# The order of an S5 branch in a three-branch token mixer: tables in two places, scan beside other products

## The chip, the cores and the metric

The kernel runs on one core of a Trainium2 chip. The metric is the device time of one execution in microseconds. TensorE has two clock levels, 1.2 and 2.4 GHz; the profile gives the granted clock as a share of full speed.

## The reference

One layer of a diffusion backbone: 256 latent tokens and 256 context tokens of width 2048, weights in fp32. Both are modulated, projected by one wide matrix `w_in`, and go through three branches of width 768: Hyena (long convolution), mLSTM (scores and states over chunks of 64), and S5 (a complex diagonal state space model). The branches are gated, merged, projected by `w_out`, normalised, and a squared-ReLU MLP of width 8192 follows. The change concerns the S5 branch:

```
SPLIT_SIZES = ((HY_ORDER + 1) * W_HY, 2 * W_ML, W_ML, W_ML, 4 * ML_HEADS, W_S5, N_BRANCH * D_MODEL)
mag = jnp.exp(dt * a_re)
ab_re, ab_im = mag * jnp.cos(dt * a_im), mag * jnp.sin(dt * a_im)
...
bu_re = jnp.einsum('blgc,gpc->blgp', u, bb_re)          # and bu_im
_, _, s_re, s_im = lax.associative_scan(s5_combine, (a_re, a_im, bu_re, bu_im), axis=1)
y = (jnp.einsum('blgp,gcp->blgc', s_re, c_re) - jnp.einsum('blgp,gcp->blgc', s_im, c_im))
```

It runs forward and backward, with 48 groups of 16 channels and 64 states.

## The kernel before

**Weights.** Every matrix streams from HBM in chunks of 512 KB (`wr`, four buffers, SP's queue). ScalarE copies a chunk to a high part `wh` (L190), VectorE makes the low part `wl` by subtraction (L194), three buffers each; TensorE then does three matmuls of 256 columns per 128 x 128 piece (L211), hi x hi, hi x lo, lo x hi, into the PSUM tile `mm`. 24 such matmuls per chunk and token stream, 192 per block of a latent projection.

**Order.** After each chunk `chunk_done` (L216) advances up to three generators, `sides[0]` to `sides[2]`, at a rate given with each. A scheduler then fixes the order on every engine from a timeline of its own. So the rates and the order of calls in `run` set what stands beside what, loosely.

**Stages.** First the modulation blocks (L394), the modulated activations (`h_group`, L427) and parts of the K projection, with `s5_params` (L440) and `s5_tables` (L540) as side. Then V, Q, `mlstm`, U (the S5 inputs), O, 36 chunks of the hyena columns HY, 96 chunks of the merge gates MG, hyena, three merges, `w_out` and the MLP.

**S5.** The sequence is cut into 32 chunks of 8 tokens for each of the two streams. `s5_tables` makes powers times B (`WA`, into the state), powers times C (`QD`, out of the state) and a short kernel (`KK`), 6 column tiles x 2 halves x 2 directions; `powers` (L524) is four multiplications and an addition, on VectorE for the forward and on GpSimd for the backward direction. Tables go to DRAM. `s5_spread` (L594) lays `KK` out as `KD` by eight DMAs of GpSimd's queue. `s5_inject` (L616) multiplies inputs by `WA`; `s5_scan` (L645) runs 63 steps of four operations on GpSimd, each dependent on the one before; `s5_output` (L658) multiplies states by `QD` (L687) and inputs by `KD` (L693), for six column tiles; GLU follows. Before, inject starts after six chunks of HY, the scan runs beside the rest of HY and MG, and the output step stands beside MG. B, C and the powers stay in SBUF while the tables are made.

**Names.** `aux` is a PSUM tile with two buffers; `b2`, `b4`, `t32`, `ty`, `t6` are SBUF tiles by size; `s5Q`, `s5t`, `s5w` are tables being made; `s5wq` and `s5tp` hold tables read back; `sc1`, `sc2` are the scan's temporaries; `mac` is the accumulator of the late modulation, VectorE's work on `wr` (L1181).

## Time and profile before

| | us |
|---|---|
| three runs | 2031.67, 2040.69, 2040.85; median 2040.69 |
| profiled execution, its own time | 2046.25 |
| its span | 2044.3 |
| TensorE busy | 1885.0 (92%) |
| VectorE busy | 1342.6 (66%) |
| ScalarE busy | 797.7 (39%) |
| GpSimd busy | 473.4 (23%) |
| moved from and to HBM | 455.92 MB, mean 223 GB/s |

The last matmul of K ends at 235.0 us and V's first starts at 242.2; V ends at 335.8, Q at 383.7, U at 459.8, O at 520.6, HY at 662.4, MG at 1049, the merges at 1177, `w_out` at 1274, the first MLP product at 1479, the second at 2028. The scan lasts from 634.4 to 807, the output step to 858.

Busy shares are averages; the trace is to be read by stages. Idle time of an engine that is not the last one waited for costs nothing.

### The profile page before, as it was taken

The page shows a single profiled execution, that of the slowest core. Times are in us where ns is not written, and L with a number is a line of the kernel's source. Part 1 is how long each engine was busy: PE and PEld are TensorE (multiplying, and loading weights), DVE is VectorE, ACT ScalarE, POOL GpSimd, SP SyncE. Part 2 cuts the span into 40 slices and gives each one's busy share as a digit, 9 for nine tenths or more (in the row PEclk, how much of TensorE's full clock was granted, in tenths as well). Part 3 has the DMA queues.
Part 4 walks back from the last instruction along what each step waited for, and adds up shares of the span by engine and source line. Part 5 has one row for each costly group of instructions (what it writes and reads, how often), then busy time and mean ns, then how long its engine had stood idle before and what let it go on. Part 6 is the DMA issues. An engine that isn't in the chain of part 4 may idle for free.

```text
span 2044.3 us, 34693 instructions
## 1 busy us (share of the span) xinstructions
PE 1885.0 (92%) x13945; PEld 1716.5 (84%) x13945; DVE 1342.6 (66%) x1842; ACT 797.7 (39%) x1079; POOL 473.4 (23%) x654
## 2 busy tenths in 40 slices
PE   4787899999999896999889998899999999999996
PEld 1555888898998896999769977899989899998986
DVE  8789876655876564455777767866655555555556
ACT  1233333324544332534333443544343334444332
POOL 4777311000015997000343400500000000000001
PEclk8898899999999898999999999999999999999998
DMA  8798667766698675777756876577765566666653
GB/s 311 262 299 285 195 203 221 228 199 184 206 318 272 211 242 172 262 251 243 270 183 217 278 249 218 174 248 229 244 208 190 189 185 181 184 185 230 190 187 115
DMA packets 255200, 455.92 MB, mean 223 GB/s; under 512 B 28789, under 2 KB 75541, under 8 KB 253504
## 3 DMA queue, kind: packets, MB, share of 16 engines
q1 hardware_dynamic: 221824, 382.43, 59.0%
q0 software_dynamic: 12384, 44.54, 6.2%
q10 hardware_dynamic: 20832, 26.75, 3.9%
q8 instruction: 109, 1.79, 0.4%
q14 instruction: 51, 0.42, 0.1%
HBM read 424.75 MB, written 32.05 MB: 223 GB/s over the span
## 4 chain that ended last, share of the span: by engine, by line
PE 64%; DVE 14%; DMA 8%; POOL 8%; issue 4%; ACT 1%; ACTq 0%; POOLq 0%; DVEq 0%; SPq 0%
PE mm L211 57%; DMA wr<-in_w_mod_dram 4%; PE aux L211 4%; DVE wl L194 4%; POOL sc L654 2%; POOL sc L653 2%; POOL t L655 2%; POOL sc L652 2%; DVE t L194 1%; DMA wr<-in_w_in_dram 1%; DVE ty L435 1%; ACT wh L190 1%; DVE mac L1181 1%; DVE s5t L537 1%; DMA s5wq<-WA 1%
## 5 line engine op out<-in xcount | busy, mean ns | idle before, releaser
L211 PE MATMUL mm<-t,wh 128*128 128x256 f32 x5888 | 1102.7, 288 | 24.8 <-ACT wh L190 12.6
L211 PEld LDWEIGHTS mm<-t,wh 128*128 128x128 f32 x5888 | 933.7, 194 | 46.6 <-ACT wh L190 13.9
L194 DVE TENSOR_TENSOR wl<-wr,wh 128x1024 fp32r<-128x1024 f32 (+1 forms) x517 | 657.0, 1277 | 381.6 <-ACT wh L190 380.7
L211 PE MATMUL mm<-t,wl 128*128 128x256 f32 x2944 | 850.1, 289 | 23.3 <-DVE wl L194 23.0
L190 ACT ACTIVATE wh<-wr 128x1024 fp32r<-128x1024 f32 (+1 forms) x517 | 546.4, 1058 | 807.9 <-PE mm L211 577.6
L211 PEld LDWEIGHTS mm<-t,wl 128*128 128x128 f32 x2944 | 571.4, 194 | 37.4 <-DVE wl L194 29.4
L1181 DVE SCALAR_TENSOR_TENSOR mac<-wr,vecs,mac 128x512 f32<-128x512 f32 x240 | 186.8, 778 | 152.7 <-DMA wr<-in_w_mod_dram 150.0
L211 PE MATMUL mm<-wh,t 128*128 128x512 f32 (+1 forms) x960 | 249.3, 349 | 1.7 <-ACT wh L190 1.7
L211 PEld LDWEIGHTS mm<-wh,t 128*128 128x128 f32 x960 | 169.7, 191 | 25.6 <-ACT wh L190 2.7
L211 PE MATMUL mm<-wl,t 128*128 128x512 f32 (+1 forms) x480 | 169.2, 352 | 5.2 <-DVE wl L194 5.2
L211 PE MATMUL mm<-wh,ff 128*128 128x512 f32 (+1 forms) x576 | 155.3, 358 | 0.0
L211 PEld LDWEIGHTS mm<-wh,ff 128*128 128x128 f32 x576 | 101.8, 188 | 17.6
L211 PEld LDWEIGHTS mm<-wl,t 128*128 128x128 f32 x480 | 91.6, 191 | 21.7 <-DVE wl L194 10.5
L211 PE MATMUL mm<-wl,ff 128*128 128x512 f32 (+1 forms) x288 | 103.0, 357 | 0.0
L1403 POOL DMA_DIRECT2D t<-in_ln_g_dram x1 | 0.5, 535 | 358.8 <-PE mm L211 358.8
L211 PE MATMUL mm<-ty,wh 128*128 128x256 f32 x384 | 74.1, 291 | 0.0
L211 PE MATMUL mm<-ty,wl 128*128 128x256 f32 x192 | 57.0, 297 | 6.7 <-DVE wl L194 6.7
L211 PEld LDWEIGHTS mm<-ty,wh 128*128 128x128 f32 x384 | 61.6, 195 | 0.9
L211 PEld LDWEIGHTS mm<-wl,ff 128*128 128x128 f32 x288 | 54.2, 188 | 8.8
L1192 POOL DMA_DIRECT2D mrow<-b x8 | 4.0, 502 | 227.8 <-DVE b L1190 227.8
L211 PE MATMUL aux<-t,t 128*128 128x384 f32 (+3 forms) x160 | 48.8, 422 | 8.0 <-DVE t L1147 3.5
L406 PE MATMUL px<-wr,b 128*32 128x512 f32 x128 | 40.3, 714 | 12.9 <-DVE s5t L335 10.7
(389 smaller groups left out, 1813.6 us busy)
## 6 DMA issues: line engine op xcount, KB each, us to landing
wr<-in_w_ff_dram SPq DMA_DIRECT2D x256, 512.0 KB, 3.9
wr<-in_w_in_dram SPq DMA_DIRECT2D x192, 512.0 KB, 4.7
wr<-in_w_mod_dram SPq DMA_DIRECT2D x160, 512.0 KB, 4.8
wr<-in_w_out_dram SPq DMA_DIRECT2D x32, 512.0 KB, 4.9
wh<-in_w_mod_dram SPq DMA_DIRECT2D x16, 512.0 KB, 6.2
wl<-in_w_mod_dram SPq DMA_DIRECT2D x16, 512.0 KB, 7.8
QD<-s5Q POOLq DMA_DIRECT2D x24, 256.0 KB, 4.9
WA<-s5wa ACTq DMA_DIRECT2D x24, 256.0 KB, 5.2
```

Source lines behind the costliest of these rows:

```text
L190: return self.nc.scalar.activation(out, in_, f, bias=bias, scale=scale)
L194: self.nc.vector.tensor_sub(lo, x, hi.bitcast(F32))
L211: self.nc.tensor.matmul(out, lhsT, rhs, start=start, stop=stop, skip_group_check=True)
L406: nc.tensor.matmul(ps[o:o + 32], self.st[:, k, :], raw[:, kk, :], start=k < 4, stop=k >= KT - 4, skip_group_check=True, tile_position=(0, o))
L435: self.nc.vector.tensor_scalar(h[:, j], h[:, j], self.modc[:, 16 + k, m:m + 1], self.modc[:, k, m:m + 1], op0=ALU.mult, op1=ALU.add)
L537: e.tensor_mul(t[:, :, s], bcp(s), bcm(1))
L652: v.tensor_mul(t1, self.a8[:, 0], S[:, :, :, :, n - 1])
L653: v.tensor_mul(t2, self.a8[:, 1], S[:, :, ::-1, :, n - 1])
L654: v.tensor_add(t1, t1, S[:, :, :, :, n])
L655: v.tensor_add(S[:, :, :, :, n], t1, t2)
L1181: v.scalar_tensor_tensor(acc, x, c, acc, op0=ALU.mult, op1=ALU.add)
L1192: nc.gpsimd.dma_start(self.mrow[which // 3:which // 3 + 1, o:o + 512], brow)
```

## The change

It is one rearrangement with these parts:

- `h_group` modulates on ScalarE instead of VectorE.
- In the first stage only `s5_params` and a new `s5_into` run. It makes `WA`, all on VectorE, four groups at once: 12 units of four multiplications of 512 elements per partition and one addition of 1024. B and the powers are written to DRAM (`SB`, `PQ`).
- `s5_spread` and the small copy `gate` ahead of it leave the place before V.
- The order is V, U, Q, mLSTM, O, HY, MG. `s5_inject` runs as side beside Q, with `WA` loaded in pieces of 256 KB; `s5_scan` is a side from mLSTM on. mLSTM calls `chunk_done`, and its scores lie in four `ty` tiles instead of one `t32`.
- `s5_tables`, now only the `QD` and `KK` part, runs as side beside all 36 chunks of HY. It loads B, the powers and C with GpSimd's queue, and makes 12 units of four multiplications of 576 and one addition of 1152, on VectorE alone. `QD` and `KK` are written by ScalarE's queue, and `s5_spread` stands at the end of it.
- `s5_output` stands beside the first 12 chunks of MG. The inputs in SBUF (`uT`) are replaced by a DRAM copy `UL`, read back on ScalarE's queue for each column tile.

```
-                    self.nc.vector.tensor_scalar(h[:, j], h[:, j], self.modc[:, 16 + k, m:m + 1],
-                                                 self.modc[:, k, m:m + 1], op0=ALU.mult, op1=ALU.add)
+                    self.act(h[:, j], h[:, j], AF.Identity, bias=self.modc[:, k, m:m + 1],
+                             scale=self.modc[:, 16 + k, m:m + 1])
...
-        e = self.nc.vector if d == 0 else self.nc.gpsimd
+        v = self.nc.vector
+        q = slice(24 * d + 4 * ct, 24 * d + 4 * ct + 4)
...
+            v.tensor_mul(out[:, s], bcp(1 + s), bcm(0))
+            v.tensor_mul(t[:, s], bcp(s), bcm(1))
+        v.tensor_add(out, out, t)
+
+    def s5_into(self):
...
+        for ct in range(CT):
+            wt = []
+            for d in range(2):
+                w = self.t(self.br, [P, 2, 4, P], "s5w", 4)
+                self.powers(w.rearrange("p s q (l c) -> p s q l c", c=16), self.s5B, d, ct, d, LC)
...
     def s5_tables(self):
+        nc.gpsimd.dma_start(B.rearrange("p a b c -> p (a b c)"), self.SB)
+        nc.gpsimd.dma_start(self.pq.rearrange("p a b c -> p (a b c)"), self.PQ)
+        nc.gpsimd.dma_start(C, self.I["s5c"])
+        yield
...
+                Q = self.t(self.br, [P, 2, 4, 144], "s5Q", 2)
+                self.powers(Q.rearrange("p s q (l c) -> p s q l c", c=16), C, d, ct, 0, 9)
...
+                nc.scalar.dma_start(self.QD[ct, d], Q[:, :, :, o:o + P])
...
-            nc.gpsimd.dma_start(self.KK[ct], kk.rearrange("p l c -> p (l c)"))
+            nc.scalar.dma_start(self.KK[ct], kk.rearrange("p l c -> p (l c)"))
             yield
+        self.s5_spread()
...
-            self.nc.vector.tensor_copy(self.uT[:, ct, :], ps[:, 2 * c + 1, :])
+            ul = self.b2([P, T])
+            self.nc.vector.tensor_copy(ul, ps[:, 2 * c + 1, :])
+            self.nc.scalar.dma_start(self.UL[ct], ul)
...
+            ul = self.b2([P, T])
+            nc.scalar.dma_start(ul, self.UL[ct])
...
-                gate = self.t(self.sm, [P, LC], "gate", 1)
-                nc.gpsimd.tensor_copy(gate[:LC], self.kT[:LC, 2, :LC])
-                nc.gpsimd.dma_start(self.KD[:, 0, 0, 0, 0].unsqueeze(1), gate[:LC, 0:1])
-                self.s5_spread()
...
+                self.lin_w_all(w_in, O_U, W, KT, both, self.u_consume)
+                self.drain(2)
                 self.qT = self.t6([P, CT, T])
                 self.sides[1][1] = 0.3
+                self.with_side(self.s5_inject(), 2)
                 self.lin_w_all(w_in, O_Q, W, KT, lat, self.q_consume)
+                self.drain()
+                self.sides[1][1] = 0.6
+                self.with_side(self.s5_scan(), 2)
                 self.mlstm()
...
+            with self.scope("pT") as self.br:
+                self.with_side(self.s5_tables(), 1, 2)
+                self.run_steps(hy, 37)
+                self.drain(2)
+                self.drain()
             with self.scope("pB") as self.br:
-                self.n6 = 5
-                hy = self.lin_w_steps(w_in, O_HY, 3 * W, KT, lat, self.hy_consume)
-                self.run_steps(hy, 6)
-                self.s5_inject()
-                self.sides[1][1] = 0.3
-                self.with_side(self.s5_scan(), 2)
-                self.run_steps(hy, 36)
-                self.run_steps(steps, 32)
                 self.with_side(self.s5_output(), 0.6)
-                self.run_steps(steps, 48)
+                self.run_steps(steps, 12)
                 self.drain()
                 self.s5_glu()
```

GpSimd, in the kernel before, at its start (`s5par`, `s5B`, `s5C` are the S5 inputs, `s5bb` a small table with zeros):

```order
L445 DMA s5par_27_119<-in_s5a_dram 128x144
L447 DMA s5B_28_121<-in_s5b_dram 128x1536
L448 DMA s5C_29_122<-in_s5c_dram 128x1536
L554 MEMSET s5bb_48_308 128x128
L554 MEMSET s5bb_51_329 128x128
```

GpSimd, in the changed kernel, in the scan's 56th step (the lines L666 to L669 are a step's four operations; L1111 belongs to the hyena inputs):

```order
L667 TENSOR_TENSOR sc2_839_5837<-t32_480_3691 128x96
L668 TENSOR_TENSOR sc1_838_5836<-sc1_838_5836,t32_480_3691 128x96
L1111 DMA HX_17_93<-b2_843_5860 256x1x128
L669 TENSOR_TENSOR t32_480_3691<-sc1_838_5836,sc2_839_5837 128x96
L570 DMA s5B_775_5466<-SB_7_78 128x1536
L571 DMA s5pq_777_5468<-PQ_8_79 128x1296
L572 DMA s5C_776_5467<-in_s5c_dram 128x1536
L581 MEMSET s5bb_789_5526 128x256
L581 MEMSET s5bb_805_5631 128x256
L666 TENSOR_TENSOR sc1_857_5924<-t32_480_3691 128x96
```

The load of C, and those of B and the powers that the tables now need again, stood at the head of GpSimd's work and stand behind 56 steps of the scan.

TensorE, in the kernel before, between two column tiles of the output step (L687 and L693 make `aux` of a tile, the eight L211 into `aux` bring it into its final order, `mm` is a block of MG):

```order
L211 MATMUL mm_1135_8338<-t32_20_103,wl_1187_8788 128x256
L211 MATMUL mm_1135_8338<-t32_20_103,wh_1186_8787 128x256 x2
L211 MATMUL aux_1151_8457<-consts_15_91,b4_1146_8412 128x32 x8
L687 MATMUL aux_1161_8541<-s5wq_1160_8531,b4_1145_8410 64x128 x16
L693 MATMUL aux_1161_8541<-s5tp_1159_8529,b2_1158_8527 32x128 x8
L211 MATMUL mm_1135_8338<-t32_20_103,wl_1187_8788 128x256
```

TensorE, in the changed kernel, at the same step (L703 and L709 are L687 and L693 of before):

```order
L211 MATMUL mm_1084_7651<-t32_23_106,wl_1109_7859 128x256
L709 MATMUL aux_1042_7253<-s5tp_1039_7239,b2_1038_7237 32x128 x8
L211 MATMUL aux_1043_7282<-consts_18_94,b4_1037_7235 128x32 x8
L703 MATMUL aux_1055_7372<-s5wq_1053_7360,b4_1036_7233 64x128 x16
L709 MATMUL aux_1055_7372<-s5tp_1052_7358,b2_1051_7356 32x128 x8
L211 MATMUL aux_1056_7401<-consts_18_94,b4_1037_7235 128x32 x8
L703 MATMUL aux_1067_7487<-s5wq_1065_7475,b4_1036_7233 64x128 x16
```

The weight matmuls into `mm` between one tile and the next have gone; the tiles follow one another directly.

VectorE, in the kernel before, in the same part of HY (L741 and L743 are the hyena columns' short convolution):

```order
L194 TENSOR_TENSOR wl_798_6128<-wr_796_6125,wh_797_6127 128x1024
L1181 SCALAR_TENSOR_TENSOR mac_677_5244<-wr_817_6251,vecs_16_93,mac_677_5244 128x512
L741 SCALAR_TENSOR_TENSOR b2_756_5918<-b4_752_5906,vecs_16_93,b2_756_5918 128x4x63
L194 TENSOR_TENSOR wl_805_6170<-wr_803_6167,wh_804_6169 128x1024
L980 SCALAR_TENSOR_TENSOR ty_634_4880<-aux_684_5283,vecs_16_93,ty_634_4880 128x256
L980 SCALAR_TENSOR_TENSOR ty_634_4880<-aux_685_5289,vecs_16_93,ty_634_4880 128x256
L1181 SCALAR_TENSOR_TENSOR mac_677_5244<-wr_817_6251,vecs_16_93,mac_677_5244 128x512
L743 SCALAR_TENSOR_TENSOR b2_756_5918<-b4_752_5906,vecs_16_93,b2_756_5918 128x4x63
L194 TENSOR_TENSOR wl_812_6212<-wr_810_6209,wh_811_6211 128x1024
```

VectorE, in the changed kernel, at the start of the tables (L537 to L539 are `powers`):

```order
L537 TENSOR_TENSOR s5Q_788_5520<-s5pq_777_5468,s5C_776_5467 128x576
L538 TENSOR_TENSOR s5t_778_5469<-s5pq_777_5468,s5C_776_5467 128x576
L537 TENSOR_TENSOR s5Q_804_5625<-s5pq_777_5468,s5C_776_5467 128x576 x2
L1198 SCALAR_TENSOR_TENSOR mac_861_5936<-wr_931_6418,vecs_19_96,mac_861_5936 128x512
L757 SCALAR_TENSOR_TENSOR b2_850_5883<-b4_840_5851,vecs_19_96,b2_850_5883 128x4x63
L539 TENSOR_TENSOR s5Q_788_5520<-s5Q_788_5520,s5t_778_5469 128x1152
L194 TENSOR_TENSOR wl_936_6437<-wr_934_6434,wh_935_6436 128x1024
L194 TENSOR_TENSOR wl_939_6476<-wr_937_6473,wh_938_6475 128x1024
```

The units of the tables stand between the splits of the weights, on the engine that makes `wl` for TensorE.

## Rows read from the trace of the kernel before

**Rows 1.** Windows: length, busy us of PE, PEld, DVE, ACT, POOL; clock, DMA share, GB/s.

```profile
0.00:242.00 242.00, 176.05 (x1248) 123.45 (x1249) 204.69 (x347) 73.95 (x187) 146.93 (x205) 0.87 0.82 274
...
20.00:40.00 20.00, 13.09 (x66) 3.69 (x66) 19.45 (x59) 3.32 (x14) 8.49 (x15) 0.74 0.98 360
200.00:220.00 20.00, 10.51 (x68) 8.09 (x59) 19.84 (x28) 7.63 (x16) 12.00 (x17) 0.66 0.64 197
...
242.00:592.00 350.00, 347.75 (x2712) 321.70 (x2710) 242.60 (x468) 137.23 (x214) 29.84 (x44) 1.00 0.69 214
592.00:864.00 272.00, 237.98 (x2236) 231.70 (x2235) 149.58 (x201) 108.12 (x166) 169.27 (x278) 0.93 0.73 242
...
635.00:809.00 174.00, 141.84 (x1122) 139.25 (x1123) 95.27 (x93) 59.01 (x70) 163.61 (x269) 0.91 0.66 213
...
972.00:1177.00 205.00, 183.22 (x1358) 172.12 (x1359) 160.60 (x189) 81.60 (x105) 82.00 (x82) 0.96 0.72 238
```

**Rows 2.** 0:242 by line: L536, L537, L538 (VectorE, GpSimd), L435 (VectorE), L564 (TensorE, loads).

```profile
0.00:242.00 242.00, 36.04 (x48) 40.49 (x48) 0.87 0.82 274
...
0.00:242.00 242.00, 35.10 (x48) 38.16 (x48) 0.87 0.82 274
...
0.00:242.00 242.00, 28.82 (x24) 34.44 (x24) 0.87 0.82 274
...
0.00:242.00 242.00, 21.57 (x32) 0.87 0.82 274
...
0.00:242.00 242.00, 17.93 (x192) 10.68 (x192) 0.87 0.82 274
```

**Rows 3.** Waits in 592:864: us in total, times, longest.

```profile
PE aux L687 <- POOL sc L652: 15.8, 1, 15.8
```

**Rows 4.** Chain of waits, start and length in us.

```profile
27.05 0.67 DVE s5Q L538
```

**Rows 5.** All transfers in 0:240.

```profile
DMA packets 36473, 66.26 MB, mean 276 GB/s; under 512 B 2689, under 2 KB 11025, under 8 KB 36456
```

**Rows 6.** Chain of waits, KD's issues, then one column tile of the output step.

```profile
252.83 2.79 POOL KD L598 x4
...
824.59 1.71 PE aux L211 x16
826.29 1.90 PE aux L687 x32
828.19 0.57 PE aux L693 x16
828.76 3.79 PE mm L211 x30
```

**Rows 7.** Line L652, the scan's first operation: ns min/median/max.

```profile
L652 POOL TENSOR_TENSOR sc<-t x63: 433/446/1302, 634.4 to 806.8; 128x96 f32<-128x96 f32 x63
```

**Rows 8.** Transfers: KB each and median us to landing.

```profile
KK<-s5kk POOLq DMA_DIRECT2D x6, 120.0 KB, 4.6
...
KD<-KK POOLq DMA_DIRECT2D x8, 384.0 KB, 8.5
...
s5tp<-KD ACTq DMA_DIRECT2D x4, 512.0 KB, 8.1
```

**Rows 9.** Costliest groups of the page: busy, mean ns of one, idle before.

```profile
L194 DVE TENSOR_TENSOR wl<-wr,wh 128x1024 fp32r<-128x1024 f32 (+1 forms) x517 | 657.0, 1277 | 381.6 <-ACT wh L190 380.7
L1181 DVE SCALAR_TENSOR_TENSOR mac<-wr,vecs,mac 128x512 f32<-128x512 f32 x240 | 186.8, 778 | 152.7 <-DMA wr<-in_w_mod_dram 150.0
...
L211 PE MATMUL aux<-t,t 128*128 128x384 f32 (+3 forms) x160 | 48.8, 422 | 8.0 <-DVE t L1147 3.5
```

**Rows 10.** Lines L190 (copies, by shape) and L702, 800:864 and whole.

```profile
L190 ACT ACTIVATE b<-t x24: 293/310/315, 806.7 to 843.9; 64x128 f32<-64x128 f32 x24
L190 ACT ACTIVATE b<-aux x24: 373/375/377, 812.4 to 854.0; 32x256 f32<-32x256 f32 x24
...
L702 DVE SCALAR_TENSOR_TENSOR z<-ty,vecs,aux x6: 682/684/735, 818.4 to 858.2; 128x256 f32<-128x256 f32 x6
```

More of the change, by code (lines that the diff above doesn't have):

```diff
@@ L445, in s5_params @@
         nc.gpsimd.dma_start(par, I["s5a"])
-        B, C = (self.t(self.br, [P, 2, 48, 16], tag, 1) for tag in ("s5B", "s5C"))
+        B = self.t(self.br, [P, 2, 48, 16], "s5B", 1)
         nc.gpsimd.dma_start(B, I["s5b"])
-        nc.gpsimd.dma_start(C, I["s5c"])
         yield
         are, aim, lg = par[:, 0, :], par[:, 1, :], par[:, 2, :]
-        self.work = [self.t(self.br, [P, 1152], f"s5t{d}", 1) for d in range(2)]
-        tmp = self.slices(self.work[0][:, :1104].rearrange("p (a n) -> p a n", n=48))
+        self.work = self.t(self.br, [P, 1152], "s5t", 1)
+        tmp = self.slices(self.t(self.br, [P, 23, 48], "s5tmp", 1))
         dt_, mag, ph, cs, sn = (tmp(x) for x in ("dt", "mag", "ph", "cs", "sn"))
@@ L503, in s5_params @@
         br, bi = B[:, 0], B[:, 1]
-        w1, w2 = (self.work[1][:, 384 * i:384 * i + 384].rearrange("p (q c) -> p q c", c=16) for i in range(2))
+        w1, w2 = (self.work[:, 384 * i:384 * i + 384].rearrange("p (q c) -> p q c", c=16) for i in range(2))
         for d in range(2):
@@ new lines, in s5_tables @@
+            for d in range(2):
+                q = slice(24 * d + 4 * ct, 24 * d + 4 * ct + 4)
+                Q = self.t(self.br, [P, 2, 4, 144], "s5Q", 2)
+                self.powers(Q.rearrange("p s q (l c) -> p s q l c", c=16), C, d, ct, 0, 9)
+                bb = self.t(self.br, [P, 2, 4, 32], "s5bb", 2)
+                nc.gpsimd.memset(bb, 0.0)
+                for h in range(2):
+                    for s in range(2):
+                        self.act(bb[64 * h:64 * h + 64, s, :, 16 * h:16 * h + 16],
+                                 B[64 * h:64 * h + 64, s, q, :], scale=1.0 - 2.0 * s)
+                yield
+                l0 = 0 if d == 0 else 16
+                for s in range(2):
+                    for p in range(4):
+                        nc.tensor.matmul(pk[32 * p:32 * p + 32, d, :], bb[:, s, p, :], Q[:, s, p, l0:l0 + P],
+                                         start=d == 0 and s == 0, stop=s == 1, skip_group_check=True,
+                                         tile_position=(0, 32 * p))
+                o = 16 - l0
+                nc.scalar.dma_start(self.QD[ct, d], Q[:, :, :, o:o + P])
@@ L687, in s5_output @@
                         self.nc.tensor.matmul(py[o:o + 64, p // 2, :], xb[:, p, d, s].rearrange("p g j -> p (g j)"),
-                                              Q[:, d, p, s, :], start=p < 2 and d == 0 and s == 0, stop=False,
+                                              Q[:, d, s, p, :], start=p < 2 and d == 0 and s == 0, stop=False,
                                               skip_group_check=True, tile_position=(0, o))
@@ L1414, in run @@
         self.WA = self.t(self.dr, [CT, P, 4, 4, P], "WA")
-        self.QD = self.t(self.dr, [CT, 2, P, 4, 2, P], "QD")
+        self.QD = self.t(self.dr, [CT, 2, P, 2, 4, P], "QD")
+        self.SB = self.t(self.dr, [P, 1536], "SB")
+        self.PQ = self.t(self.dr, [P, 1296], "PQ")
+        self.UL = self.t(self.dr, [CT, P, T], "UL")
         self.mrow = self.t(self.dr, [2, D], "mrow")
@@ L1470, in side @@
                     yield from self.s5_params()
-                    yield from self.s5_tables()
+                    yield from self.s5_into()
                 self.with_side(side(), 1.0)
```

124 lines of the change are left out of this document (50 added, 74 removed).

## The prediction

> **What bounds the kernel now.** I read the time by stages first [rows 1], because the share of busy time over the whole span mixes stages with different limits. Reading the busy columns of each line, TensorE fills 347.75 of 350 us from V to O and nearly as much later, so there only work taken off TensorE would count. Three stretches have room. The first 242 us (modulation blocks, modulated activations, S5 tables, K) hold only 176.05 us of matmuls, and VectorE is busy for 204.69. The stretch 592:864 (inject, scan, start of the S5 output) has 237.98 of 272. The stretch with hyena, 972:1177, has 183.22 of 205. Then I split the first stretch by line [rows 2]: the table multiplications cost VectorE 36.04 + 35.10 + 28.82 = 100 us, the modulation L435 21.57, and GpSimd works beside it on as many tables. Last I read what holds TensorE in 592:864: one wait of 15.8 us [rows 3] of the first output matmul (L687) on the scan.
>
> **K stage: -54.** The change takes 100 + 21.57 us off VectorE and puts 12 units of `s5_into` there: four multiplications of 512 elements and one addition of 1024. A 576-element operation took 0.67 us in a quiet place [rows 4], so 512 take 0.60 and 1024 1.19: 12 x (4 x 0.60 + 1.19) = 43. VectorE is left with 204.69 - 121.5 + 43 = 126 us. TensorE loses the table matmuls, 17.93 of 176.05, and has 158. ScalarE gets the 32 modulations, which at VectorE's mean (21.57 / 32 = 0.67 us) are 22 us on its 73.95: no bound. So loads become the limit: 66.26 MB in 240 us [rows 5], less the Q tables written (24 x 256 KB = 6.3 MB), one 0.8 MB load and 0.7 MB of KK, plus 1.4 MB of stored B and powers: 60 MB. In 20:40 the engines moved 360 GB/s [rows 1]; at that rate 60 MB take 167 us. Behind the last load three buffered chunks of 48 matmuls remain, at 3.79 / 30 = 0.126 us each [rows 6] 18 us. K ends at 185, V starts 3 us later, instead of at 242: -54. At 300 GB/s, K would end near 215; that is a rival. The gate copy and the KD transfers that stood ahead of V on GpSimd also go, at no further gain, since TensorE was busy nearly throughout the stage after them [rows 1].
>
> **Table matmuls: +18.** The 192 matmuls L564 cost 17.93 us [rows 2]. They now stand among the hyena columns, where TensorE has no room: +18.
>
> **Inject and scan under Q and O: -41.** In 592:864 TensorE is idle for 34 us, 15.8 of them in the one wait [rows 3], and its clock was 0.93 [rows 1], between its levels of 1.2 and 2.4 GHz. Inject now waits for pieces loaded beside Q, and the scan ends some hundred us ahead of its reader. I take the 34, and 7 for the clock (nearly half of 0.07 x 272 = 19 us, since some low clock was idle time already counted): -41. Only the 15.8 is certain.
>
> **New wait at the first table matmul: +38.** The tables need B, the powers and C, loaded by GpSimd's queue, where the built order puts the loads behind 56 of the 63 scan steps. In 635:809 GpSimd was busy 163.61 us for 63 steps, 2.60 us a step, while VectorE was busy for 95.27 [rows 1]; one operation's median is 0.446 [rows 7], so four alone are 1.78. VectorE is at least as loaded under O and the hyena columns, so I take 2.60: 56 x 2.60 = 145. Before it 3 us until the scan starts, after it 2 for three issues, 8 for the landing (KD's 8.5 [rows 8]), and 7 for the first unit on VectorE and the small copies. That is 165. Between the last inject matmul and the first table matmul TensorE has 612 weight matmuls, at 0.126 us [rows 6] 77; 88 score and state products of the mLSTM branch, at the 0.422 of the row for small products [rows 9] 37; and 38 transposes and sums with fewer columns, at two thirds of it 11. With 2 for handovers that is 127 us. 165 - 127 = +38. Ends: 56 x 1.78 = 100 gives no wait, 0; VectorE taking all it can gives 78.
>
> **VectorE as partner in the table phase: +9.** 24 + 24 multiplications at 0.67 are 32 us, 12 additions of 1152 elements at 1.34 are 16, 25 splits at 1.277 are 32, 10 accumulations at 0.778 are 8 [rows 9], and 23 short convolution and kernel operations some 5 to 10: 93 to 98 us. TensorE has 600 matmuls and the table matmuls: 76 + 18 = 94. Two engines with equal work in lock-step lose a little at each handover: 12 units of under 1 us, +9 (0 to 20).
>
> **The kernel-table chain: +10.** The Toeplitz tables now pass through KK and KD right before their use: landing of KK 4.6, eight issues at 0.70 (2.79 for four), KD 8.5, reading it 8.1 [rows 6, 8], 27 us together. The built order leaves TensorE 74 matmuls and one 22 more, and small work, for 12 to 17 of it: +10. Before, the same chain ran beside V.
>
> **The output step, now serial: +28.** Before, its six column tiles came every 7.96 us, each 1.71 + 1.90 + 0.57 of its own matmuls and 3.79 of 30 weight matmuls that filled the wait [rows 6]. In the new order no weight matmul stands among five of the six. One tile is then a ring: four copies at 0.31, 1.90 and 0.57 on TensorE, four copies at 0.375, 1.71, VectorE's 0.68 [rows 6, 10], the issue of the next load of `ul` on ScalarE's queue (which waits for that VectorE operation, and behind it stand the next tile's copies), about 0.4: 1.24 + 2.47 + 1.50 + 1.71 + 0.68 + 0.4 = 8.0, and six handovers at 0.2: 9.1. Six are 54.6, of which 25 are TensorE's own work: 29.6, less 2 for the 22 matmuls. +28.
>
> **Smaller things: +12.** GLU's activations stand open, for which I put +4, an estimate of some ten operations of ScalarE of the length of those in rows 10. At half-busy TensorE the clock falls: in 200:220 it was 0.66 at 10.51 busy of 20 [rows 1]; 4.18 us of own matmuls at 0.66 instead of 0.94 cost 1.8 more, over six tiles and the wait +8.
>
> **Hyena, merges, tail: 0.** The 22 us of idle time in 972:1177 [rows 1] have their own causes, and as many weight matmuls stand there as before.
>
> **Sum.** -54 + 18 - 41 + 38 + 9 + 10 + 28 + 12 = +20. On the profiled execution, 2046.25, that is 2066; the median of the runs is 5.6 lower: 2060.
>
> **A rule against the change.** GpSimd and VectorE both ran in 635:809, 163.61 and 95.27 us busy in 174 [rows 1], so at least 85 us overlapped, but a scan step took 2.60 us instead of 1.78. The Trainium skill ("SBUF — State Buffer", section "SBUF: two separate sides") says that a VectorE operation with two inputs in SBUF and a GpSimd operation that reads SBUF take a shared port pair as an exclusive lock, the loser blocked for the whole instruction. By that rule, with every VectorE operation, a GpSimd chain would go on only in the time left; the overlap shows it doesn't hold for all of them here.
>
> **Rivals.**
> - *The scan is not held up.* Then the loads go out after 100 + 3 us and land before TensorE asks: no +38, 2022. For it: the median operation of 0.446 us, and the two long table phases no longer collide with the scan's end. Against: 2.60 us a step. It decides from a step below 2.0 us.
> - *The output step and the chains hide better* than a row-by-row reading says: of the last four costs (9, 10, 28 and 12, together 59) half is paid, 29 less: 2031, about no change. For it: the rings of two tiles may overlap, since copies and loads of the next tile need nothing of this one. Against: the issue of `ul`, which stands between them on ScalarE.
> - *The K stage stays bound by loads and their splits*, at 300 GB/s or by VectorE's order: K ends at 212 instead of 185, +27, 2087. For it: the mean of 276 GB/s [rows 5] even where VectorE was not the limit.
> - *GpSimd is locked out by VectorE in the scan.* 56 x 1.78 + 85 = 185 instead of 145: +40, 2100. The overlap in 635:809 [rows 1] speaks against it.
>
> **Chances.** Forecast 0.34 (0.30 of it slower by over 0.5%, 0.04 within), scan not held up 0.26 (faster), the better hiding 0.20 (0.06 faster, 0.14 within), loads 0.14 and lock 0.06 (slower). A difference of 0.5%, 10 us, is about what a measurement can tell from none. Faster 0.32, within 0.18, slower 0.50. Signs are split, so: the forecast's own range is 2035 to 2088; the range for all cases, leaving out the lock (0.06) and the outer halves of the first rival and of the loads, is 2010 to 2088.
>
> **What would show it.** In the trace of the changed kernel: K's last matmul at 185 (right), past 205 (wrong); four scan operations at 2.6 us a step, and TensorE's wait at the first table matmul 38 us long or absent; six output tiles 9 us apart with no weight matmul between; idle time of TensorE under Q and O near nothing. The prediction is wrong if the scan step is under 2 us, or if the weight matmuls do fill the output step.

## The result and the profile after

The changed kernel takes 2091.22 us in the median against 2040.11: the ratio is 1.0266, 95% interval 1.0245 to 1.0288, some 54 us slower (51 between the medians). The profiled execution has a span of 2088.1 us against 2044.3, 43.8 more, since that of the kernel before lies 6 us above its median; the ledgers below are made against that. The forecast was 2060 with a range to 2088: slower was right, the size was not.

The windows of the changed kernel, to be read beside [rows 1] (length; busy us of TensorE, weight loads, VectorE, ScalarE, GpSimd with instructions; granted clock; DMA share; GB/s):

```profile
0.00:201.00 201.00, 159.02 (x1057) 112.27 (x1058) 121.47 (x252) 69.15 (x112) 8.65 (x32) 0.89 0.88 300
201.00:422.00 221.00, 218.32 (x1802) 201.82 (x1801) 151.13 (x306) 64.80 (x94) 15.31 (x29) 1.00 0.73 228
422.00:493.00 71.00, 67.19 (x568) 54.95 (x567) 38.53 (x68) 27.88 (x49) 36.85 (x67) 0.98 0.67 213
493.00:519.00 26.00, 17.57 (x75) 14.25 (x74) 17.64 (x42) 12.58 (x34) 24.12 (x49) 0.76 0.20 61
519.00:666.00 147.00, 126.39 (x1046) 122.01 (x1046) 113.25 (x163) 65.77 (x119) 93.56 (x157) 0.94 0.63 197
666.00:703.00 37.00, 31.10 (x301) 28.47 (x299) 34.63 (x52) 16.22 (x39) 4.54 (x9) 0.95 0.74 213
703.00:810.00 107.00, 69.83 (x552) 63.94 (x550) 31.79 (x58) 31.49 (x68) 12.11 (x18) 0.67 0.63 224
810.00:868.00 58.00, 51.20 (x361) 47.40 (x362) 41.50 (x54) 22.32 (x33) 18.18 (x19) 0.94 0.69 237
868.00:1108.00 240.00, 227.73 (x1814) 221.56 (x1813) 150.16 (x163) 88.81 (x100) 40.55 (x43) 0.99 0.72 230
```

V's first matmul stands at 201.0 instead of 242.2, so the K stage gave 41 us. Two lines stand out among those that give them back. In 493:519 TensorE is busy for 17.57 of 26 us at a clock of 0.76, and the DMA engines move 61 GB/s: the weights stand still while mLSTM's state products run. In 703:810 it is busy for 69.83 of 107 at 0.67: the output step.

Both kernels have 11916 weight matmuls, in the same sequence of products but for U and Q. So one can ask in each trace when the n-th of them ended:

| n-th weight matmul | before, us | after, us | difference | what lies between |
|---|---|---|---|---|
| 576 | 235.0 | 193.9 | -41.1 | K stage |
| 1152 | 335.8 | 292.0 | -43.8 | V |
| 2448 | 547.3 | 544.9 | -2.5 | U, Q, O, mLSTM; after also inject |
| 3312 | 689.8 | 687.1 | -2.7 | rest of HY; before inject, after the tables |
| 3600 | 727.5 | 823.4 | +95.9 | after output step and GLU |
| 6000 | 1121.0 | 1168.9 | +47.9 | before has made up the output step, GLU; both hyena |
| 11900 | 2026.0 | 2069.1 | +43.1 | merges, MLP |

At n = 3312 and at n = 6000 both kernels have about the same side work behind them. So the gain of 44 is used up in the middle (+41), and the part with output step, GLU and hyena adds 51. Single executions differ by some 5 us in such a stretch: in e9_late, whose code is that of the kernel before up to n = 3312, n = 1152 to 3312 take 349.4 us, here 353.9.

Of the 51 us, half are idle time and half are products that take longer. The stretch n = 3312 to 6000 in the kernel before, then in the changed one:

```profile
689.80:1121.00 431.20, 388.23 (x3209) 373.04 (x3210) 267.73 (x307) 168.69 (x227) 177.29 (x260) 0.96 0.69 228
```

```profile
687.10:1168.90 481.80, 413.10 (x3262) 394.37 (x3263) 275.47 (x341) 176.25 (x247) 83.52 (x99) 0.91 0.71 232
```

TensorE is idle for 68.7 us instead of 43.0, and busy for 413.1 instead of 388.2 at a granted clock of 0.91 instead of 0.96.

The output step, matmuls of TensorE in the changed kernel (start, length, what, and in brackets the idle time ahead and who ended it):

```profile
744.02 1.08 PE L709 MATMUL aux<-s5tp,b 128*32 128x128 f32 x16 [17.81 <-DMA s5tp<-KD]
746.93 3.60 PE L211 MATMUL aux<-consts,b 128*128 128x32 f32 x16 [1.83 <-ACT b L190]
750.46 3.68 PE L703 MATMUL aux<-s5wq,b 128*64 128x128 f32 x32
754.07 1.08 PE L709 MATMUL aux<-s5tp,b 128*32 128x128 f32 x16
756.90 1.97 PE L211 MATMUL aux<-consts,b 128*128 128x32 f32 x16 [1.75 <-ACT b L190]
...
789.41 0.86 PE L709 MATMUL aux<-s5tp,b 128*32 128x128 f32 x16
```

The kernel table `s5tp` comes 17.81 us late; then six tiles follow one another, (789.41 - 744.02) / 5 = 9.08 us apart, with no weight matmul between. The same products that took 1.71 and 1.90 us in [rows 6] take up to 3.60 and 3.68. The clock of the two halves, from windows of the same kernel:

```profile
700.00:744.00 44.00, 19.56 (x146) 17.98 (x145) 22.05 (x36) 12.32 (x22) 12.11 (x18) 0.71 0.99 362
744.00:794.00 50.00, 39.39 (x351) 35.35 (x351) 8.01 (x21) 15.23 (x41) 0.56 (x1) 0.64 0.50 168
```

In the first the DMA engines are busy for 0.99 of the time, at 362 GB/s. There the eight transfers of KD stand (issues of line L611 and their landing, us):

```profile
L611 POOL DMA_DIRECT2D KD<-KK x8: 731/733/777, 712.8 to 717.9; - x8
...
DMA to landing us min/median/max: 8.0/14.1/19.7
```

They landed in 8.5 us in [rows 8] and now take 14.1, while weights and Q tables move as well.

### The profile page after: what moved, and what is told of

It is laid out like the page before. It is cut to its first block, busy times and chain, and to the rows that moved or that the text cites. A ratio compares the mean times of both kernels' runs of the same rounds, so it can differ in the third digit from the quotient of the medians.

```text
span 2088.1 us, 34595 instructions
## 1 busy us (share of the span) xinstructions
PE 1904.7 (91%) x13945; PEld 1728.8 (83%) x13945; DVE 1302.5 (62%) x1810; ACT 803.5 (38%) x1063; POOL 330.2 (16%) x494
## 4 chain that ended last, share of the span: by engine, by line
PE 42%; DMA 6%; DVE 5%; issue 1%; ACT 1%; POOL 0%; POOLq 0%; DVEq 0%; ACTq 0%
PE mm L211 42%; DMA wr<-in_w_mod_dram 3%; DVE wl L194 2%; DMA wr<-in_w_out_dram 1%; DVE t L194 1%; ACT wh L190 1%; DMA wr<-in_w_s_out_dram 1%; DVE mac L1198 1%; DMA wr<-in_w_hy_out_dram 0%; DMA mg<-MG 0%; PE px L211 0%; POOL t L1252 0%; DMA wr<-in_w_ff_dram 0%; DVE x L1407 0%; DVE t L1150 0%
## 5 line engine op out<-in xcount | busy, mean ns | idle before, releaser
L211 PE MATMUL mm<-t,wh 128*128 128x256 f32 x5888 | 1109.3, 289 | 42.1 <-ACT wh L190 29.2
L211 PEld LDWEIGHTS mm<-t,wh 128*128 128x128 f32 x5888 | 938.0, 195 | 69.2 <-ACT wh L190 33.3
L194 DVE TENSOR_TENSOR wl<-wr,wh 128x1024 fp32r<-128x1024 f32 x517 | 646.7, 1254 | 455.6 <-ACT wh L190 448.6
L190 ACT ACTIVATE wh<-wr 128x1024 fp32r<-128x1024 f32 x517 | 546.0, 1058 | 866.8 <-PE mm L211 599.6
L211 PE MATMUL mm<-t,wl 128*128 128x256 f32 x2944 | 852.0, 290 | 16.9 <-DVE wl L194 16.9
L211 PEld LDWEIGHTS mm<-t,wl 128*128 128x128 f32 x2944 | 573.6, 195 | 30.8 <-DVE wl L194 23.4
L211 PE MATMUL mm<-wh,t 128*128 128x512 f32 (+1 forms) x960 | 247.6, 347 | 0.2 <-ACT wh L190 0.2
L211 PEld LDWEIGHTS mm<-wh,t 128*128 128x128 f32 x960 | 168.3, 189 | 23.7 <-issue 0.9
L211 PE MATMUL mm<-wl,t 128*128 128x512 f32 (+1 forms) x480 | 167.8, 350 | 4.9 <-DVE wl L194 4.8
L211 PE MATMUL mm<-wh,ff 128*128 128x512 f32 (+1 forms) x576 | 153.9, 356 | 0.0
L211 PEld LDWEIGHTS mm<-wh,ff 128*128 128x128 f32 x576 | 101.2, 188 | 17.4
L211 PEld LDWEIGHTS mm<-wl,t 128*128 128x128 f32 x480 | 90.9, 189 | 20.4 <-DVE wl L194 9.2
L211 PE MATMUL mm<-wl,ff 128*128 128x512 f32 (+1 forms) x288 | 102.4, 356 | 0.0
L211 PE MATMUL mm<-ty,wh 128*128 128x256 f32 x384 | 69.9, 284 | 0.0
L211 PE MATMUL mm<-ty,wl 128*128 128x256 f32 x192 | 55.2, 287 | 8.1 <-DVE wl L194 7.9
L211 PEld LDWEIGHTS mm<-wl,ff 128*128 128x128 f32 x288 | 54.1, 188 | 8.7
L211 PEld LDWEIGHTS mm<-ty,wh 128*128 128x128 f32 x384 | 59.9, 192 | 0.1
L211 PE MATMUL aux<-t,t 128*128 128x384 f32 (+3 forms) x160 | 47.2, 410 | 12.7 <-DVE t L1153 4.5
L666 POOL TENSOR_TENSOR sc<-t 128x96 f32<-128x96 f32 x63 | 36.6, 581 | 81.0 <-DVE t L655 76.2
```

The lines of the kernel that those rows point to most:

```text
L190: return self.nc.scalar.activation(out, in_, f, bias=bias, scale=scale)
L194: self.nc.vector.tensor_sub(lo, x, hi.bitcast(F32))
L211: self.nc.tensor.matmul(out, lhsT, rhs, start=start, stop=stop, skip_group_check=True)
L666: v.tensor_mul(t1, self.a8[:, 0], S[:, :, :, :, n - 1])
```

## The experiments

Each ratio is against the kernel before, on the same chip; the changed kernel's is 1.0266. "Back" is the difference of the two ratios in us (0.01 is 20.4 us).

**e1_fill: weight matmuls beside the output step.**

```
-                self.with_side(self.s5_output(), 0.6)
-                self.run_steps(steps, 12)
+                self.with_side(self.s5_output(), 0.3)
+                self.run_steps(steps, 24)
```

> The changed kernel, with 24 merge-gate chunks beside the output step instead of 12 (its generator at rate 0.3), so that 24 to 30 weight matmuls stand in each ring and 142 ahead of the first one. Theory A (chains of small steps without cover beside them): TensorE's 39 us of idle time in 703:830 fall below 10 and the output products get their clock back, 40 to 50 us less than the changed kernel's 2091, so 2041 to 2051. Rival B (the weights' supply through ScalarE and VectorE sets the pace there, the waits come back later): less than 15 us gained, 2076 or more.

Ratio 1.0073 (1.0048 to 1.0097), 2052.16 us: 39 us back. Windows of this kernel from the last tables to the end of GLU:

```profile
704.00:750.00 46.00, 32.55 (x238) 30.13 (x228) 23.15 (x38) 14.45 (x24) 12.11 (x18) 0.85 1.00 360
750.00:804.00 54.00, 49.03 (x552) 46.15 (x551) 27.15 (x43) 30.41 (x58) 2.70 (x5) 0.97 0.86 306
```

With weight matmuls in the rings (24 to 33 in each, and still only 7.98 us from tile to tile) TensorE is busy for 49.03 of 54 us at 0.97, and the output products are back at their length. Theory A holds for this place, though just short of its numbers: 39 us where 40 to 50 were expected, and 18.8 us of idle time left in 703:830 where fewer than 10 were.

**e12_cover: weight matmuls only ahead of it.**

```
+                self.run_steps(steps, 8)
                 self.with_side(self.s5_output(), 0.6)
                 self.run_steps(steps, 12)
```

> The changed kernel with eight more merge-gate chunks ahead of the output step: 125 weight matmuls (15 us at 0.126) stand ahead of the first use of the kernel table instead of 22, and 30 in the first two or three rings; the other rings stay bare. If the wait for the kernel table (17.8 us) and the bare rings are separate costs, this returns 14 to 25 of the 39 us that e1_fill returned: 2066 to 2077. If the table's transfers only land later because the weights' loads are in their way, under 8 us.

Ratio 1.0173 (1.0154 to 1.0192), 2073.7 us: 19 us back, as expected for two separate costs. In the built order 125 weight matmuls stand ahead of the first use of the kernel table, 30, 30 and 14 in the first three rings, none in the others. TensorE's wait for `s5tp` is gone, and so is half of its waits in the rings (5.3 us instead of 10.6). So the 19 us are the price of the wait and of some of the rings; the run doesn't tell the two apart.

**e5_inter2: HY's chunks between mLSTM's blocks.**

```
-                self.chunk_done()
+                self.run_steps(self.hy, 2)
                 num = self.b4([P, HEADS, DH + 1])
```

> The changed kernel, with two chunks of the hyena columns written out after each of the four blocks of mLSTM's decayed scores, so that 63, 16 and 57 weight matmuls stand between the blocks of state products (0, 17 and 53 before) and none is missing at the end of O. Theory A: the 26 us without a weight matmul at 493:519 go (TensorE was idle for 8 of them, and its 18 busy ones ran at a clock of 0.76), 10 to 18 us less than the changed kernel, 2073 to 2081. Rival D (the products only move, their cost is their own length and the idle time comes back as a wait for the scan-delayed tables): less than 5 us gained.

Ratio 1.0270 (1.0242 to 1.0297): nothing back. The n-th matmul at n = 2448 is 6.5 us earlier than in the changed kernel (538.4 for 544.9, although V started 5 us later), but at n = 3312 the gain is 1.7 us and at n = 3600 it is gone. The wait moved: to the tables, and then to a Q table that is late at the output step (waits of TensorE in 420:870):

```profile
PE aux L709 <- DMA s5tp<-KD: 14.3, 1, 14.3
...
PE aux L703 <- DMA s5wq<-QD: 10.5, 1, 10.5
...
PE aux L591 <- DVE s5Q L539: 4.5, 1, 4.5
```

The result is that of rival D: mLSTM's gap and the scan's chain run at the same time, and to shorten the gap alone returns nothing that the runs can tell from none.

**e3_ldq: the tables' inputs by SP's queue.**

```
-        nc.gpsimd.dma_start(B.rearrange("p a b c -> p (a b c)"), self.SB)
+        nc.sync.dma_start(B.rearrange("p a b c -> p (a b c)"), self.SB)
```

(likewise for the powers and C)

> The changed kernel, with B, the powers and C loaded by SP's queue instead of GpSimd's, so not behind 56 scan steps. Theory A: the one wait for them (ScalarE 17.8 us on B's landing, TensorE 13.3 us behind it) goes: 10 to 15 us less, 2076 to 2081. Rival C: the tables then run beside the scan on VectorE, the scan step goes from 2.5 us to 3 or more, and nothing or less than 5 us is gained.

Ratio 1.0224 (1.0199 to 1.0249): 9 us back, with intervals that just overlap the changed kernel's. The first table matmul stays at 605.8 (606.4). In the changed kernel ScalarE waited for the load of B, here for the zeroed table that GpSimd makes behind the same scan; the two rows are from the changed kernel and from this one:

```profile
ACT s5bb L190 <- DMA s5B<-SB: 17.8, 1, 17.8
```

```profile
ACT s5bb L190 <- POOL s5bb L581: 29.6, 4, 17.1
```

So it was not a test of the term: two things stood behind the scan, and one was moved. What returned the 9 us is open: counted from V's start, the n-th matmul is 3.6 us earlier at n = 3312, 7 at 6000 and 10 at 11900, with no one place.

**e11_fill_ldq2: both moved off GpSimd, on top of e1_fill.**

```
-                nc.gpsimd.memset(bb, 0.0)
+                v.memset(bb, 0.0)
```

> The changed kernel with the merge-gate chunks beside the output step (e1_fill), the tables' inputs loaded by SP's queue, and the small zeroed tables made by VectorE, so that nothing of the tables waits on GpSimd's queue behind the scan. Theory: the first table matmul, at 606 in the changed kernel with the loads on either queue, comes 15 to 25 us earlier; the scan's last steps slow down beside the tables, but nobody waits for them. 10 to 20 us less than e1_fill: 2032 to 2042. Rival: VectorE, with splits, accumulations, short convolutions and tables, is the limit there, and under 5 us are gained.

Ratio 1.0051 (1.0035 to 1.0067), 2049.28 us: 4 us less than e1_fill, with overlapping intervals. The first table matmul comes at 595.7 (with V's start 3.5 us later than in the profiled changed kernel, so some 14 us earlier); the last one comes at 704, no earlier. The tables now take 108 us instead of 94; in 650:704 VectorE is busy for 49.81 of 54 us. The gain is the rival's; that VectorE's work sets the end of the tables fits, but was not tested apart.

**e14_half_after: half of the scan's steps left out.**

```
-        for n in range(1, NCH):
+        for n in range(1, NCH // 2):
```

> The changed kernel with 31 instead of 63 scan steps, so that 31 instead of 56 steps stand ahead of the loads of the tables' inputs. If the loads behind the scan hold the middle (the prediction's +38), the first table matmul comes 20 to 40 us earlier than 606 and the total falls by 15 to 35 us, to 2056 to 2076. If mLSTM's products and VectorE's own order hold it, the total stays within 10 us of 2091.

Ratio 1.0150 (1.0105 to 1.0195), 2068.93 us: 24 us back. The first table matmul stands at 587.1 and the last one at 682.9, 17 us earlier than 700.4 (line L591: ns min/median/max, first to last start):

```profile
L591 PE MATMUL aux<-s5Q,s5bb x192: 269/273/364, 587.1 to 682.9; 128*32 128x128 f32 x192
```

So the tables did hang on the scan, for 17 to 24 us of it, not 38. The edit takes away two things at once, the scan's place ahead of the loads and its work beside VectorE. e11_fill_ldq2, where the loads and zeroed tables are free of the scan but the scan runs on, has its last table matmul no earlier, so the place in the queue alone is not the whole price. The gap at 493:519 is still there.

**e13_half_before: the same in the kernel before.** (The edit is that of e14_half_after.)

> The kernel before with 31 instead of 63 scan steps (the other half of the states is left as injected). The scan then ends some 80 us earlier and nothing waits for it. If the prediction's -41 was right, all idle time of TensorE in 592:864 goes and the run is 30 to 41 us faster, 1998 to 2009; if only the row of 15.8 us was the scan's, 12 to 20 us, 2019 to 2027.

Ratio 0.9923 (0.9896 to 0.9950), 2018.04 us: 16 us faster than the kernel before, 10 to 21 by the interval. That is about the one wait row of [rows 3], and well below 30. (The two profiled executions lie 30.6 us apart, but that of the kernel before is above its median and this one below its own.) TensorE in 592:864, then its waits in 592:1049:

```profile
592.00:864.00 272.00, 258.57 (x2421) 252.80 (x2421) 153.59 (x212) 116.88 (x177) 92.18 (x152) 0.96 0.79 262
```

```profile
PE mm L211 <- DVE wl L194: 11.8, 9, 2.6
PE mm L211 <- ACT wh L190: 9.6, 3, 5.4
```

These two were in the kernel before too, with 14.4 and 9.2 us, and hardly change when half of the scan goes. Of the 34 us of idle time in 592:864, 13.4 stay, and the clock is 0.96 instead of 0.93.

**e9_late: a later reader in the kernel before.**

```
-                self.run_steps(steps, 32)
+                self.run_steps(steps, 40)
                 self.with_side(self.s5_output(), 0.6)
-                self.run_steps(steps, 48)
+                self.run_steps(steps, 40)
```

> The kernel before, with the output step eight merge-gate chunks later (40 instead of 32 ahead of it), so that the scan has ended when TensorE asks for the states. The term of the prediction at stake is -41 for what scan and inject cost TensorE in 592:864. If all of its idle time there came from their place, 30 us or more go; if only the wait rows that name them are theirs (15.8 for the scan, 1.9 for inject), 12 to 18 us, 2019 to 2025; if the wait only moves to the end of the merge gates, less than 5.

Ratio 0.9997 (0.9984 to 1.0010): no change, the case in which the wait only moves. The row of 15.8 us is gone from TensorE and stands on VectorE, which waits for the scan's last step with the weights' splits queued behind it (TensorE in 592:1049, then VectorE in 740:830):

```profile
PE mm L211 <- DVE wl L194: 30.0, 9, 21.0
```

```profile
DVE b L680 <- POOL t L655: 22.4, 1, 22.4
```

**e2_uback: the old order, V, Q, mLSTM, U, O.** Inject runs beside O and the scan beside HY and the tables; tables, K stage and output step are as in the changed kernel.

```
-                self.lin_w_all(w_in, O_U, W, KT, both, self.u_consume)
                 ...
-                self.with_side(self.s5_scan(), 2)
                 self.mlstm()
+                self.lin_w_all(w_in, O_U, W, KT, both, self.u_consume)
                 ...
+                self.with_side(self.s5_inject(), 2)
                 self.lin_w_all(w_in, O_O, W, KT, lat, o_consume)
```

> The changed kernel, with the old order V, Q, mLSTM, U, O; inject beside O, scan beside the hyena columns. Tables, output step and K stage as in the changed kernel. Theory A: the 26 us between the last product of O and the first of HY, in which mLSTM's state products run one after another, go, and V to HY takes 285 to 295 us instead of 318: 20 to 30 us less, 2061 to 2071, unless the later scan delays the tables' loads. Rival B (the state products need that time anyway and appear in O): within 8 us of 2091.

Ratio 1.0473 (1.0442 to 1.0504), 2135.71 us: 42 us slower than the changed kernel, so neither theory. The gap of mLSTM did not go, it moved in front of U: Q's last matmul ends at 344.7 and U's first starts at 382.7. In the kernel before, mLSTM's state products lay at 488.8 to 546.2, among the matmuls of O and HY; here they run from 380.9 on, right behind Q. The scores' four `ty` tiles in place of one `t32` may be what lets them; that was not tested. And the scan beside the tables became slower (line L666, then the zeroed tables that wait behind it):

```profile
L666 POOL TENSOR_TENSOR sc<-t x63: 427/535/1432, 547.9 to 766.5; 128x96 f32<-128x96 f32 x63
```

```profile
ACT s5bb L190 <- POOL s5bb L581: 79.6, 9, 12.1
```

(766.5 - 547.9) / 62 = 3.53 us a step. The run says nothing on the price of the old order by itself.

**e4_into1: one of six column tiles of the input tables.**

```
-            wt = []
-            for d in range(2):
+            if ct == 0:
+                wt = []
+                for d in range(2):
```

> The changed kernel, making only the first of the six column tiles of the input tables (the other five write the first one's tables again, so transfers and TensorE's work are the same and the results are not the reference's). It takes some 35 us of VectorE's work out of the K stage. If loads bound that stage, K's last product moves by less than 4 us from 193.9; if VectorE or the hand-over between engines still bounds it, by 8 us or more, and the total with it.

Ratio 1.0236 (1.0212 to 1.0260), 6 us back, with intervals that overlap; K ends at 192.2, 1.7 us earlier than in the changed kernel, where the runs with this stage unchanged have 193.9 to 201.4. That is the first expectation: VectorE's tables no longer bound the K stage.

**e7_hgdve: the modulations back on VectorE.** (The first four lines of the change undone.)

> The changed kernel with the 32 modulations back on VectorE. VectorE has room in the K stage now (121 of 201 us), so by the reading that loads and the last group's chain bound it, K ends within 5 us of 193.9 and the total is within 8 us of 2091. If VectorE still bounds it, K ends 15 us later or more.

Ratio 1.0250 (1.0233 to 1.0267): no difference to the changed kernel that is clear of noise, and K ends at 189.2, no later. In it the move to ScalarE is worth nothing: VectorE has time there.

**e8_hgact: only that move, in the kernel before.**

> The kernel before, with only the 32 modulations moved from VectorE to ScalarE. VectorE is busy for 204.69 of its first 242 us, so if VectorE alone bounds the stage, K ends up to 21.6 us earlier, 2016 to 2025; if the split halves of the tables on GpSimd (147 us) and the handing-over bound it too, 3 to 10 us.

Ratio 0.9944 (0.9924 to 0.9964), 2022.76 us. V's first matmul comes at 231.8 instead of 242.2. So some 10 us, half of the 21.6 that VectorE loses, are gained: VectorE is a limit there, and not the only one.

**e6_combo: e1_fill, e3_ldq and e5_inter2 together.**

> The changed kernel with the merge-gate chunks beside the output step (as in e1_fill), the chunks of the hyena columns between mLSTM's blocks (as in e5_inter2), and the tables' inputs on SP's queue (as in e3_ldq). Theory A (separate places, so the gains add up): -39, -8 and -10 to -18 from 2091 give 2026 to 2034, just faster than the kernel before. Rival B (each fills its wait with work that is then missing later): 2045 or more.

Ratio 1.0097 (1.0069 to 1.0124): no better than e1_fill alone. The gains don't add up, as e5_inter2 says: against e1_fill the n-th matmul is 14 us earlier at n = 2448 and 2 at n = 3312.

**e10_hglate: e8_hgact and e9_late together.**

> The kernel before, with the modulations on ScalarE (as in e8_hgact) and the later output step (as in e9_late). The two places lie 500 us apart, so the gains should add: 13.6 from e8_hgact and 12 to 18 give 2005 to 2011, faster than both kernels. If the two share a limit (the weights' supply), 2018 or more.

Ratio 0.9923 (0.9909 to 0.9936), 2022.02 us: the fastest complete version, 0.8% faster than the kernel before, but its interval overlaps that of e8_hgact alone, as e9_late alone is worth nothing.

**e15_hgearly and e16_hgearlylate: the scan started earlier.**

```
-                self.run_steps(hy, 6)
+                self.run_steps(hy, 1)
                 self.s5_inject()
```

> The kernel before with the modulations on ScalarE (e8_hgact) and the injection one chunk into the hyena columns instead of six, so that the scan starts some 12 us earlier against the same reader. If the scan's length is the limit there, 8 to 12 us less than e8_hgact's 2023: 2011 to 2015. If the mLSTM's work ahead of it sets the scan's start, no change.

> The same with the injection ahead of the hyena columns and the reader eight merge-gate chunks later. Start and reader together would cover the wait of 16 us: 2005 to 2010. If VectorE again takes the wait over, 2015 to 2022.

0.9986 (0.9970 to 1.0002) and 0.9966 (0.9951 to 0.9982): both gain less than e8_hgact (0.9944), which they contain. Up to n = 6000 their profiled executions are 0.4 and 2.4 us ahead of it; 10 and 15 us are lost behind that, in stages that the edits don't touch, and the runs are from another chip. Why was not found. The scan's first step stood at 619.5 and 619.2, where e8_hgact has 619.3, so the injection's new place did not move its start. What holds its start was not tried.

## Why the prediction was wrong in size

The prediction's terms, put on the stretches of the table of n-th matmuls. The text doesn't split the -41; here it goes by the kernel before, where TensorE was busy for 84.56 of 97.8 us at 0.90 in 592:689.8 and for 153.42 of 174.2 at 0.95 in 689.8:864. That is 13 of the 34 us of idle time and some 4 of the 7 for the clock ahead of n = 3312, 21 and 3 behind it:

| stretch | forecast | measured |
|---|---|---|
| K stage and V | -54 | -43.8 |
| middle, n = 1152 to 3312 | 18 + 38 + 9 - 17 = +48 | +41.1 |
| output step, GLU, MG, hyena, n = 3312 to 6000 | 10 + 28 + 12 - 24 = +26 | +50.6 |
| rest | 0 | -4.8 |
| sum | +20 | +43.1 |

**The step that failed is "Inject and scan under Q and O: -41".** It booked all idle time of TensorE in 592:864 and a part of the low clock as the scan's. e13_half_before takes the scan's hold away and returns 16 us (10 to 21), about the one row of [rows 3]. The other waits in that stretch (on `wl` and `wh`) stay there, and stay in e9_late too. The text said that only 15.8 was certain, and then took 41.

With 16 the sum is +45, where the profiled runs differ by 43.8, but that it fits so closely is luck. The wait of 15.8 us lay behind n = 3312, so the forecast becomes 18 + 38 + 9 = +65 for the middle and 10 + 28 + 12 - 16 = +34 for the stretch behind it: 24 us too much and 17 too little. With the K stage's 10 and the 5 of the rest the errors cancel.

**K stage, -54.** Right in kind, 10 to 13 us too large. In 0:160 the DMA engines were busy for 0.94 of the time at 325 GB/s, and e4_into1 shows VectorE's tables not to bound it; so loads did, until the last chunks (windows of the changed kernel):

```profile
140.00:160.00 20.00, 19.76 (x149) 15.55 (x149) 4.29 (x5) 1.66 (x2) 0.00 (x0) 0.97 0.89 307
160.00:180.00 20.00, 13.32 (x87) 10.69 (x87) 11.86 (x16) 10.02 (x17) 1.67 (x3) 0.74 0.71 223
180.00:200.00 20.00, 20.00 (x172) 19.65 (x171) 14.90 (x25) 8.91 (x12) 0.55 (x1) 1.00 0.63 198
```

From 160 on the DMA share falls and the last group's chain (modulate, split, 144 matmuls) goes on to 193.9; I had put 18 us behind the last load. The mean rate to 201 was 300 GB/s, not 360. After K another 7 us pass until V starts, as before; I had 3.

**Table matmuls, +18.** Too large. TensorE takes 16 of them in 0.65 us where nothing holds them up:

```profile
700.07 0.65 PE L591 MATMUL aux<-s5Q,s5bb 128*32 128x128 f32 x16
```

12 x 0.65 = 7.8 us. The 17.93 of [rows 2] were the same matmuls in 24 pieces of eight, and a piece of eight took 0.61 to 1.07 us, as long as one of 16 here.

**The wait behind the scan, +38.** The scan was sized right: its steps from 453.6 to 609.3 are (609.3 - 453.6) / 62 = 2.51 us each (forecast 2.60), and the loads go out at 587.7, 134 us after its start (forecast 145). The first table matmul came 154 us after the last one of inject (452.3 to 606.4; forecast 165). But TensorE waited for only some 13 us of them, for weights queued behind ScalarE's 17.8 us on B, because its own 127 us had become longer. mLSTM's products hold TensorE for 26.3 + 19.8 = 46 us, where the text had 37 from a row that is mostly of other stages; and there is the gap of 26 us at 493:519, with idle time and a clock of 0.76, which the prediction didn't name at all. e5_inter2 shows why the sum was hardly hurt by that: the two run side by side. e14_half_after gives the scan's second half, its place in the queue and its work beside VectorE together, 17 to 24 us.

**VectorE as partner, +9.** The tables took 94 us from first to last (606.4 to 700.4). The forecast was 94 of TensorE's own work and 9 for the partner; TensorE's work was shorter by the 10 us of the line above, it was busy for 86.68 us of the stretch and VectorE for 87.82. VectorE's share is not to be had apart. In e11_fill_ldq2 an earlier start doesn't end them earlier.

**The kernel-table chain, +10.** Under-sized. From the last table matmul to the first use of KD it is 744.0 - 700.7 = 43 us, where 27 were summed up: KD's transfers land after 14.1 instead of 8.5, and their first issue comes 12 us after the last table matmul. TensorE waits for 17.8.

**The output step, +28.** The size came out, 9.08 us per tile (forecast 9.1), but by luck. Of the links of the forecast ring, TensorE waits for one alone, the copies behind L709 (1.8 us a tile); L703 of the next tile stands right behind L211, so its loads, its copies and VectorE's operation were done beside. What these links did not take, the products did: 4.18 us a tile by [rows 6], some 7.2 here (39.39 us busy in 50 us, five and a half tiles) at a clock of 0.64. That clock the prediction had priced apart, as +8 of the smaller things. e1_fill shows the step and the chain ahead of it to be worth 39 us together.

**Smaller things, +12.** GLU's part was too small: from the last tile (794.5) to GLU's last matmul (821) it is 26 us, with 23 weight matmuls of MG (2.9 us) among them, where GLU took 13.3 in the kernel before; so some 10, not 4. The low clock of the tiles is in their 9.08 us already; what it also cost, and was not named, are the weight matmuls in 700:744, at 0.71.

**The rivals.** "The scan is not held up" fell: 2.51 us a step. "Hide better" was half right: the rings of two tiles do overlap, but the low clock took what that saved. Of "stays bound by loads" the rate came (300 GB/s), not its price: K ended at 193.9, not 212 (and 60 MB at that rate with 18 us behind are 218, where the text has 215 and 212).

"Locked out" fell by its price: the 56 steps took 134 us, not 185. But the prediction read the records wrongly where it took overlapping busy times as a sign against a lock. In the changed kernel a scan step of four operations takes 2.51 us; in e2_uback, beside the table multiplications, 3.53, while these take 0.991 us in the median instead of 0.754. There, on VectorE and GpSimd:

```profile
579.34 0.94 DVE L537 TENSOR_TENSOR s5Q<-s5pq,s5C 128x576 f32<-128x576 f32 x1
579.75 0.83 POOL L666 TENSOR_TENSOR sc<-t 128x96 f32<-128x96 f32 x1
580.21 0.99 DVE L538 TENSOR_TENSOR s5t<-s5pq,s5C 128x576 f32<-128x576 f32 x1
580.54 0.95 POOL L667 TENSOR_TENSOR sc<-t 128x96 f32<-128x96 f32 x1
```

L666 starts inside L537 and ends 0.30 us after it; L538 starts inside L666 and ends 0.62 us after it. All 48 scan operations of that run that start inside a table multiplication end 0.25 to 0.31 us after it, whether they started 0.10 or 0.60 us into it, and all 48 multiplications that start inside a scan operation end 0.60 to 0.62 us after it. In the changed kernel the same holds for the 25 scan operations that start inside a split (L194). So in these pairs the second operation gets on only when the first is done, and the time in which it is held is part of its recorded length (a scan operation takes 0.433 us alone and 0.66 to 0.97 here). In 548:724 of e2_uback GpSimd is busy for 166.78 of 176 us and VectorE for 134.43, but much of that is one held by the other. The rule of the Trainium skill ("SBUF — State Buffer", section "SBUF: two separate sides"), an exclusive lock for the whole instruction on the side of whichever starts first, agrees with these pairs. What was wrong in the rival is the sum: it put all of VectorE's overlapping time on the scan.

## What to carry to other kernels

Idle time in a stretch is not yet the price of what one wants to move out of it: take the wait rows that name the moved work, and leave the rest where it is. A step that is moved loses the work beside it as well; look in the built order for what stands between its instructions on TensorE at the new place (here nothing in the rings of six tiles, and nothing for 26 us between mLSTM's blocks). A chain of small steps (load, copy, product, copy) costs its whole length there, and here most of that length was products at the low clock: 9.08 us a tile when bare, 7.98 with 24 to 33 weight matmuls in each ring, which so cost nothing. And a forecast whose terms sum up right is not yet right: look at each stretch.

## What the runs showed of the hardware that was not expected

- The scan's step depends on what VectorE does beside it: 1.78 us by the median of its operations [rows 7], 2.51 beside splits and mLSTM, 3.53 beside table multiplications with two inputs. The trace shows how: of a scan operation and such a VectorE operation the second gets on when the first is done, and the wait is recorded as busy time. So overlapping busy times of these two engines are no sign that they run side by side.
- The granted clock follows bare stretches closely: 0.64 in 744:794, where TensorE shows as busy for 39.39 of 50 us, since the same products take up to twice as long; in e1_fill the same tiles run at 0.97. Busy time alone would not have shown the loss.
- Eight transfers of 384 KB took 14.1 us in the median (up to 19.7) in a stretch with the DMA engines at 0.99, and 8.5 in the kernel before, in one at 0.77 (250:275).
